# Two low parts by adding transfers, the output projection from its other half first, and another order of the second MLP chunk

## The chip, the cores and the metric

The kernel runs as one program on one core of a Trainium2 chip. Its time is the device time in microseconds (us) of one execution. Weights and activations come from device memory; layout changes of the inputs are made on the host before and are not timed. The names of the engines in the profile are PE (TensorE, matmuls), PEld (its weight loads), DVE (VectorE), ACT (ScalarE), POOL (GpSimd) and SP (SyncE, which issues most transfers).

## What is computed

A trunk of two layers over two requests, 512 and 256 tokens of 1024 features, float32. Layer 0 mixes tokens by windowed attention, layer 1 by a gated convolution of width 3; after each come an MLP with a squared ReLU (1024 to 4096 and back) and a gated embedding of the layer:

```python
for i in range(DEPTH):
    h = rms_norm(x, norm_mix[i])
    x = x + (window_attention(h, ...) if i % 2 == 0 else short_conv(h, ...))
    h = rms_norm(x, norm_mlp[i])
    x = x + jnp.square(jax.nn.relu(h @ mlp_w_up[i])) @ mlp_w_down[i]
    gate = jax.nn.sigmoid(rms_norm(x, norm_ple[i]) @ ple_w_gate[i])
    x = x + (p[i] @ ple_w_proj[i]) * gate
return rms_norm(x, final_norm)
```

The attention ends with a projection, `out @ w_o`, whose result is added to x. The change lies there, at the beginning of layer 0's MLP, and in the second chunk of both MLPs.

## The kernel before

Features lie on the 128 partitions, so x is eight blocks of 128 features by T = 768 tokens, numbered 0 to 7; H = 384 is half of the tokens. All matmuls take operands of the type float32r. To keep the accuracy, each operand is split in two: a **high part**, which is its copy in float32r, made by ACT, and a **low part**, the operand minus its high part, made by DVE. A product is then three matmuls: high by high, high by low, low by high. The groups of instructions are named by the lines that record them: L434 is the high part of a weight and L445 its low part, both 128x1024 (1024 columns hold two blocks of 512), L466 the products of seven (below), L1062 and L1166 those of the plain chunks.

**Weights.** `Weights7` holds one chunk of an up or down matrix: two raw tiles of 512 KB, which SP loads into a ring of three buffers (`fetch`, L89). In a *plain* chunk (the first two of each up matrix, `PLAIN`) the group "direct" is the first raw tile (`w11`, `w12`) and goes to the tiles `zhi` and `zlo`, of which there is one each. The group "second" is the other raw tile (`w21`, `w22`) and goes to `whi` and `wlo`, of which there are two each, shared with other weights. `high(group)` and `low(group)` make the two parts. In the other chunks a scheme of seven products in place of eight (as Strassen's) is used, which needs sums of weight blocks: `sums32` and `sums14` are two DVE additions of 128x512 each, for the groups "s32" and "s14".

**Activations.** The same scheme needs sums of x blocks m and m + 4 (`Norm7.copied`, then `Sums`: `t13` and `t42`, two DVE operations each, and `high` and `low`, twice each). `Acts` does it for the MLP's hidden blocks: `highx`, `lowx`, `t13`, `t42`, two `high`, two `low`.

**Order.** The planner of the framework orders each engine's queue by priority and an estimate of times. Inside `manual_schedule` blocks the order of ACT, PE and DVE is that of the program text. The first six blocks of the output projection (`first_head`) are left to the planner; what follows (`first_tail`, and both MLPs) is written out by hand.

**The output projection.** For block m, `output(m)` multiplies what is still missing of the heads: for m < 4 four head blocks (24 matmuls) with a weight of `w_o0`, for m >= 4 two head blocks (12 matmuls) with `w_o2` in `zhi` and `zlo`, since the rest was added during the attention (`xa`). Then `add` adds it to x, `plain_block` makes the high and low parts of x times the gain (one ACT and one DVE operation of 128x768 for m >= 4, two of 128x384 on each for m < 4), and `square` adds the block's squares to a sum. The order of the blocks is `PAIRED`: 0, 4, 1, 5, 2, 6 in `first_head` and 3, 7 in `first_tail`. After that PE computes four products `pj` for the second layer's embedding (48 matmuls), which ACT copies out.

**The first two chunks of up.** `up_first` (layer 0; layer 1 goes through the rest of `up_begun`) multiplies chunk 0 with all of x: first the half that uses "direct", then the half that uses "second". Meanwhile ACT and DVE make the reciprocal root of the mean square (`rstd_mlp`, in three steps), the sums of x blocks (`s1` to `s3`), and the parts of chunk 1 (`v`). `up_plain` does the same for chunk 1. Each result is rectified out of PSUM by DVE (`rectified`, L1021), 128x384 at a time, squared by ACT (L1024), and turned into operands by the steps of `acts_of`, which stand in the list `pend` and are taken from it by `late(n)` or in a weave. Chunk 2 is the first with seven products (`up`); its ACT copy `c` (L1225) of the first product frees PE for the third.

In `up_plain` the order of chunk 1's other work on DVE is: four steps of chunk 0's activations, then `sums32`, `sums14` and the direct split woven with the two `high` and two `low` of the activations, then the split of "s32", then the rectifications:

```python
rest, pend[:] = pend[:4], pend[4:]
weave(rest, ...)
...
sums = [] if v.plain else [v.sums32, v.sums14, lambda: v.split("direct")]
weave(norm.combine(todo.pop(0)) if todo else [], sums, pend)
...
v.split("s32")
y1, y2 = big("y1"), big("y2")
rects((0, 1), (0, 0))
squared(y1)
...
rects((1, 1), (1, 0))
```

Of the kernel before, what the change touches and what calls it, by code (L numbers as in the profile page):

```python
# [20 lines left out]
KB = D // P  # L21
# [26 lines left out]
def trunk_kernel(ctx: ExitStack, tc: tile.TileContext, a: dict, out: bass.AP):  # L48
# [38 lines left out]
    def fetch(src):  # L87
        raw = wp.tile([P, CH], F32, name="wraw", bufs=3)
        nc.sync.dma_start(raw[:, : src.shape[1]], src)  # L89
        return raw  # L90
# [80 lines left out]
    class Norm:  # L171
# [16 lines left out]
            self.square(m, xb)  # L188

        def square(self, m, xb):  # L190
            if m == 0:
                act.activation(self.acc, xb, AF.Square)
            else:
                sq = self.temp("sq")
                act.activation(sq, xb, AF.Square)
                dve.tensor_tensor(self.acc, self.acc, sq, ALU.add)
# [5 lines left out]

        aside = temp

        ready = False

        def acc_parts(self):
            ah, al = self.aside("ah", F32R), self.aside("al", F32R)
# [187 lines left out]
    class Weights7:  # L396
# [3 lines left out]
        def __init__(self, src1, src2, plain=False):  # L400
            self.plain = plain
            self.raw = [fetch(src1), fetch(src2)]
            self.w, self.parts, self.due = {}, {}, set()
            if not plain:
                self.s = [more.tile([P, CH], F32, tag=f"sum{i}", name="sum", bufs=1) for i in range(2)]
# [11 lines left out]
        def high(self, group):  # L417

            self.due.add(group)
            names = self.GROUPS[group]  # L420
            if group in ("s32", "s14"):
                src = self.s[group == "s14"][:]
            else:
                src = self.raw[group != "direct"][:, CH - 512 * len(names) :]
            n = len(names) * 512
            if group == "s32" or (self.plain and group == "direct"):
                tag = "z"
            else:
                tag = "v" if group == "w22" else None
            if tag is None:  # L430
                hi, lo = (wp.tile([P, CH], F32R, name=f"w{p}", bufs=2) for p in ("hi", "lo"))
            else:
                hi, lo = (more.tile([P, n], F32R, tag=f"{tag}{p}", name=f"{tag}{p}", bufs=1) for p in ("hi", "lo"))
            act.activation(hi[:], src, AF.Copy)  # L434
            self.parts[group] = hi, lo, src
            for i, k in enumerate(names):
                c = slice(512 * i, 512 * i + 512)
                self.w[k] = hi[:, c], lo[:, c]

        def low(self, group):  # L440
            if group not in self.due:
# [391 lines left out]
    def add(m, ps, src=None):  # L833

        src = x(m) if src is None else src
        for t, o, e in pieces(ps):
            dve.tensor_tensor(x(m)[:, o:e], src[:, o:e], t, ALU.add)
# [108 lines left out]
    def first_head(norm):  # L946


        behind, product, ws = second_inputs(xs0[24:])
        w = [weight(a["w_o0"][2], 4)] * 2  # L950
        w2 = weight(a["w_o2"], 2, tag="z")

        def output(m):
            ps = both()
            if m < KB // 2:
                group2(ps, terms_of(w[m], [p[4:] for p in aos], col=m % 2 * P))
            else:
                group2(ps, terms_of(w2, [p[6:] for p in aos], col=(m - 4) * P))
            return ps

        for i, m in enumerate(PAIRED[:6]):
            if i == 1:
                w += [weight(a["w_o0"][3], 4)] * 2
            ps = output(m)
            add(m, ps, xa[m])
            norm.block(m, x(m))
            behind(i)

        return output, product, ws

    def first_tail(norm, places, output, product, ws):

        pjs = []

        def copied(m):
            t = slot(places[m], "pjs", F32)
            for f, o, e in pieces(pjs[m]):
                act.activation(t[:, o:e], f, AF.Copy)
            nc.sync.dma_start(pj[1][KB // 2 + m], t[:])

        norm.ready = True
        c = ws[1]
        m6, m7 = PAIRED[6:]
        ps = [output(m) for m in (m6, m7)]
        pjs.extend(product(m) for m in range(KB // 2))
        add(m6, ps[0], xa[m6])
        norm.plain_block(m6, x(m6))
        norm.square(m6, x(m6))
        c.high("direct")
        add(m7, ps[1], xa[m7])  # L990
        norm.plain_block(m7, x(m7))
        c.low("direct")
        norm.square(m7, x(m7))
        copied(0)
        parts = norm.acc_parts()
        s0 = norm.copied(0, 4)
        copied(1)
        s0.t13()
        c.high("second")
        s0.high(0)  # L1000
        c.low("second")
        copied(2)
        s0.t42()
        s0.high(1)
        s1 = norm.copied(1, 5)
        copied(3)
        s0.low(0)
        s0.low(1)
        return c, up_chunk(0, 1), parts, s1

    def mlp(l, norm, nxt, w, places, early, product=None, begun=None):
# [85 lines left out]
        def up_first(ps, w, v, parts, s1):  # L1097


            nonlocal r  # L1100
            plain_block(ps[0], 0, w, range(4))
            ss = norm.sum_squares(psum, parts=parts, tag="C")
            plain_block(ps[0], 0, w, range(4, KB))
            plain_block(ps[1], 1, w)
            logs, newton, result = norm.rstd_steps(psum, ss)
            logs()
            s1.t13()
            s1.t42()
            s1.high(0)
            s1.high(1)  # L1110
            newton()
            s2 = norm.copied(2, 6)
            result()
            r = norm.r
            s1.low(0)
            s1.low(1)
            v.high("direct")
            s2.t13()
            s2.high(0)
            v.low("direct")  # L1120
            s2.t42()
            s2.high(1)
            s3 = norm.copied(3, 7)
            s2.low(0)
            s2.low(1)
            y = [big(f"y{i + 1}") for i in range(2)]
            for i in range(2):
                for o in range(2):
                    rectified(y[i], ps[i][o], H * o, H * o + H, ALU.max)
                if i == 0:  # L1130
                    s3.t13()
                    s3.high(0)
                    squared(y[0])
                    s3.t42()
                    s3.high(1)
                    v.high("second")
                    s3.low(0)
                    s3.low(1)
                    v.low("second")
            pend.extend(acts_of(0, *y, y[1]))  # L1140
            return v

        def up_plain(u, w, make, then):
# [15 lines left out]
            for n, (i, ks, sides) in enumerate(order):  # L1159
                for k in range(*ks):  # L1160
# [3 lines left out]
                    for j, (wt, part) in enumerate(((hi, 0), (hi, 1), (lo, 0))):  # L1164
                        for o in sides:
# [4 lines left out]
                                start=k == 0 and j == 0,  # L1170
                                stop=k == KB - 1 and j == 2,
                            )
                if n == 0:
                    v = make()
                    if not known and not parts:
                        parts = norm.acc_parts()
                        norm.table()
                    rest, pend[:] = pend[:4], pend[4:]
                    split2 = [lambda: v.split("second")] if v.plain else []
                    soon = v.plain and len(todo) and product  # L1180
                    weave(split2 + [lambda: v.split("direct")] if soon else [])
                    weave(rest, norm.combine(todo.pop(0)) if todo else [], [] if soon else split2)
                    if product and not known:
                        ss = norm.sum_squares(psum, parts=parts, tag="C")
                elif n == 1:
                    if not product and not known:
                        ss = norm.sum_squares(psum, parts=parts, tag="C")
                    if v.plain and not soon:
                        v.split("direct")
                    steps = [] if known else norm.rstd_steps(psum, ss)  # L1190
                    for step in steps[:1]:
                        step()
                    sums = [] if v.plain else [v.sums32, v.sums14, lambda: v.split("direct")]
                    weave(norm.combine(todo.pop(0)) if todo else [], sums, pend)
                    pend.clear()
                    for step in steps[1:]:
                        step()
                    r = norm.r
                elif n == 2:
                    if not v.plain:  # L1200
# [4 lines that stand above are left out]
                else:  # L1205
                    rects((1, 1), (1, 0))
                    pend.extend(acts_of(u, y1, y2, y2))
            return v

        def up(u, w, make, then):  # L1210
# [12 lines left out]
                late()  # L1223
            c = bank("A" if first else "C", "c")[:, :H]
            act.activation(c, a, AF.Copy)  # L1225
            late(3 if first else 1)
            w.split("w22")
            late()
            b = bank("A" if first else "B", "b")[:, :H]
# [669 lines left out]
```

## Time and profile before

| | us |
|---|---|
| median of 3 runs | 1687.13 |
| fastest and slowest of them | 1685.48, 1689.2 |
| the profiled execution, whole | 1689.38 |
| its span, first to last instruction | 1687.5 |
| output projection and `pj`, PE (layer 0) | 277 to 310.6 |
| chunk 0 of up, layer 0 | 310.8 to 328.8 |
| chunk 1 of up, layer 0 | 328.8 to 346.4 |
| chunk 2 of up, layer 0 | 346.4 to 366 |
| chunks 0, 1 of up, layer 1 | 1118.4 to 1152.5 |

How to read it: the stages are given as the times of PE's matmuls in the timeline of the profiled execution, from the span's start. A row of the timeline holds the start, the length, engine, line, operation, what is written and read, shapes and count; in brackets stand the engine's idle time before it and what ended that. A row of several instructions gives their length from the first start to the last end. The page's chain that ended last is followed back from the last instruction, at each step to what released it; its rows hold start, length, engine and tile. Matmuls overlap, so PE's idle time in the rows is somewhat less than the time lost.

### The profile page before, as it was taken

The page shows a single profiled execution, that of the slowest core. Times are in us where ns is not written, and L with a number is a line of the kernel's source. Part 1 is how long each engine was busy: PE and PEld are TensorE (multiplying, and loading weights), DVE is VectorE, ACT ScalarE, POOL GpSimd, SP SyncE. Part 2 cuts the span into 40 slices and gives each one's busy share as a digit, 9 for nine tenths or more (in the row PEclk, how much of TensorE's full clock was granted, in tenths as well). Part 3 has the DMA queues.
Part 4 walks back from the last instruction along what each step waited for, and adds up shares of the span by engine and source line. Part 5 has one row for each costly group of instructions (what it writes and reads, how often), then busy time and mean ns, then how long its engine had stood idle before and what let it go on. Part 6 is the DMA issues. An engine that isn't in the chain of part 4 may idle for free.

```text
span 1687.5 us, 24113 instructions
## 1 busy us (share of the span) xinstructions
PE 1650.1 (98%) x9410; PEld 1590.2 (94%) x9410; DVE 1415.1 (84%) x2304; ACT 903.9 (54%) x1449; POOL 18.3 (1%) x44
## 2 busy tenths in 40 slices
PE   8999999999999999999999999999999999999996
PEld 6888788989999999999999999999999999999986
DVE  6598888889999989987888877868999898998776
ACT  6377756755455455544654334545545545554544
POOL 0211000000000000000000000000000000000000
PEclk9999999999999999999999999999999999999998
DMA  8754322212221222222312222121222122122222
GB/s 261 191 153 142 95 63 82 76 63 75 66 83 64 76 71 67 74 95 72 101 60 75 76 65 77 60 74 51 75 71 80 63 76 75 63 76 88 82 75 94
DMA packets 46820, 144.60 MB, mean 86 GB/s; under 512 B 6080, under 2 KB 9152, under 8 KB 46704
## 3 DMA queue, kind: packets, MB, share of 16 engines
q1 hardware_dynamic: 45168, 139.89, 26.1%
q0 software_dynamic: 1536, 3.15, 0.8%
q8 instruction: 74, 1.21, 0.3%
q14 instruction: 42, 0.34, 0.1%
HBM read 123.10 MB, written 10.48 MB: 79 GB/s over the span
## 4 chain that ended last, share of the span: by engine, by line
PE 60%; DVE 29%; ACT 7%; issue 3%; DMA 1%; SPq 0%; DVEq 0%; ACTq 0%
PE a L466 17%; PE mm L129 9%; PE mm L138 7%; PE b L466 4%; PE gate L138 4%; PE B L466 3%; PE C L466 3%; DVE t L361 3%; DVE wlo L445 3%; DVE y L1021 3%; DVE zlo L445 2%; DVE act L394 1%; PE pt L733 1%; PE c L466 1%; ACT y L1024 1%
## 5 line engine op out<-in xcount | busy, mean ns | idle before, releaser
L434 ACT ACTIVATE whi<-sum 128x1024 fp32r<-128x1024 f32 x67 | 70.5, 1053 | 146.8 <-PE a L466 146.8
L1024 ACT ACTIVATE y<-y 128x768 f32<-128x768 f32 x64 | 53.8, 840 | 143.1 <-DVE y L1021 143.1
L466 PE MATMUL a<-xs,whi 128*128 128x384 f32 x624 | 121.9, 337 | 0.7 <-DVE low L1660 0.7
L466 PE MATMUL a<-t,zhi 128*128 128x384 f32 x536 | 109.9, 338 | 2.2 <-ACT c L1225 2.2
L466 PEld LDWEIGHTS a<-xs,whi 128*128 128x128 f32 x624 | 110.1, 188 | 1.1 <-DVE low L1660 1.1
L466 PE MATMUL a<-t,whi 128*128 128x384 f32 x536 | 108.8, 336 | 0.0
L466 PE MATMUL b<-t,zhi 128*128 128x384 f32 x536 | 108.7, 336 | 0.0
L466 PEld LDWEIGHTS a<-t,zhi 128*128 128x128 f32 x536 | 95.1, 189 | 2.7 <-ACT c L1225 2.5
L466 PE MATMUL a<-act,whi 128*128 128x384 f32 x448 | 96.6, 337 | 0.0
L445 DVE TENSOR_TENSOR wlo<-wraw,whi 128x1024 fp32r<-128x1024 f32 x72 | 87.8, 1220 | 8.7 <-ACT whi L434 8.7
L466 PEld LDWEIGHTS a<-t,whi 128*128 128x128 f32 x536 | 94.9, 188 | 0.0
L466 PEld LDWEIGHTS b<-t,zhi 128*128 128x128 f32 x536 | 94.8, 188 | 0.0
L445 DVE TENSOR_TENSOR wlo<-sum,whi 128x1024 fp32r<-128x1024 f32 x67 | 81.9, 1222 | 10.1 <-ACT whi L434 10.1
L1281 DVE TENSOR_TENSOR x<-x,a 128x384 f32<-128x384 f32 x112 | 60.8, 553 | 33.7 <-PE a L466 33.5
L434 ACT ACTIVATE zhi<-sum 128x1024 fp32r<-128x1024 f32 x67 | 71.0, 1059 | 22.8 <-DVE sum L410 22.8
L138 PE MATMUL mm<-xs_mix,whi 128*128 128x512 f32 (+1 forms) x320 | 83.1, 342 | 0.0
L445 DVE TENSOR_TENSOR zlo<-sum,zhi 128x1024 fp32r<-128x1024 f32 x67 | 81.6, 1218 | 0.0
L466 PEld LDWEIGHTS a<-act,whi 128*128 128x128 f32 x448 | 79.9, 188 | 0.0
L434 ACT ACTIVATE whi<-wraw 128x1024 fp32r<-128x1024 f32 x72 | 75.7, 1052 | 6.1 <-PE C L466 5.7
L355 ACT ACTIVATE t<-y 128x768 fp32r<-128x768 f32 x56 | 47.1, 842 | 40.3 <-DVE y L346 29.9
L466 PE MATMUL a<-xs,wlo 128*128 128x384 f32 x312 | 67.1, 336 | 0.2 <-DVE wlo L445 0.2
L466 PE MATMUL b<-t,zlo 128*128 128x384 f32 x268 | 64.1, 344 | 3.1 <-DVE zlo L445 2.0
(336 smaller groups left out, 4489.5 us busy)
## 6 DMA issues: line engine op xcount, KB each, us to landing
wraw<-in_up SPq DMA_DIRECT2D x64, 512.0 KB, 3.5
wraw<-in_down SPq DMA_DIRECT2D x64, 512.0 KB, 3.5
wraw<-in_w_in SPq DMA_DIRECT2D x24, 512.0 KB, 3.5
wraw<-in_gate SPq DMA_DIRECT2D x16, 512.0 KB, 3.5
pj<-pjs SPq DMA_DIRECT2D x16, 384.0 KB, 3.1
wraw<-in_w_q SPq DMA_DIRECT2D x8, 512.0 KB, 4.4
wraw<-in_w_out SPq DMA_DIRECT2D x8, 512.0 KB, 3.5
x_in<-in_x SPq DMA_DIRECT2D x8, 384.0 KB, 7.3
```

Of the source, the lines that this page charges most:

```text
L129: pe.matmul(t, lhsT=w, rhs=x[:, o:e], start=first and i == 0 and j == 0, stop=last and i == n - 1 and j == 2)
L138: pe.matmul(ps[:, o:e], lhsT=w, rhs=x[:, o:e], start=i == 0 and j == 0, stop=i == n - 1 and j == 2,)
L355: act.activation(t[0][:], (self.q1, self.q2)[i][:], AF.Copy)
L361: dve.tensor_tensor(lo[:], (self.q1, self.q2)[i][:], hi[:].bitcast(F32), ALU.subtract)
L394: dve.tensor_tensor(lo[:], self.q2[:], hi[:].bitcast(F32), ALU.subtract)
L434: act.activation(hi[:], src, AF.Copy)
L445: dve.tensor_tensor(lo[:], src, hi[:].bitcast(F32), ALU.subtract)
L466: pe.matmul(ps, lhsT=a, rhs=b, start=start and i == 0, stop=i == len(terms) - 1, skip_group_check=True)
L733: pe.transpose(pt[:, h * P : (h + 1) * P], lg[h // 2][:, h % 2, b * P : (b + 1) * P], ident[:],)
L1021: dve.scalar_tensor_tensor(t[:, o:e], src, 0.0, r[:, o:e], op, ALU.mult)
L1024: act.activation(t[:], t[:], AF.Square)
L1281: dve.tensor_tensor(t[:, o : o + H], t[:, o : o + H], f, op)
```

## The change

It has three parts.

1. `first_head` and `first_tail` take the blocks in the order 4, 0, 5, 1, 6, 2, then 7, 3, where it was 0, 4, 1, 5, 2, 6, then 3, 7. The first block's squares start the sum, whichever block it is (`begun`).
2. A new function, `added(group)`, makes the two parts of a weight without DVE: ACT makes the high part, ACT writes the negated high part into the low tile, and POOL issues a transfer that reads the raw weight from device memory once more (512 KB) and adds it to the low tile. It takes the place of `high` and `low` for "second" of chunk 0 in `first_tail` (now ahead of the last block's parts; before among the first sums of x) and for "second" of chunk 1 in `up_first` (now right behind the reciprocal root; before at the end, between the rectifications).
3. In `up_plain`, chunk 1 of both layers has its own order: `sums32` ahead of the hidden blocks' parts, the direct split and the split of "s32" between their steps, the first rectifications ahead of the last `high`, `sums14` behind them, and the last two `low` steps handed on to chunk 2, which takes them by `late(5)` in place of `late(3)`.

```diff
 def square(self, m, xb):
-    if m == 0:
+    if not self.begun:
+        self.begun = True
         act.activation(self.acc, xb, AF.Square)
...
 class Weights7:
         self.raw = [fetch(src1), fetch(src2)]
+        self.src = src1, src2
...
+    def added(self, group):
+        self.high(group)
+        self.due.remove(group)
+        hi, lo, _ = self.parts[group]
+        act.activation(lo[:], hi[:].bitcast(F32), AF.Copy, scale=-1.0)
+        nc.gpsimd.dma_start(lo[:], self.src[group == "second"], accum_op=ALU.add)
...
 # first_head
-for i, m in enumerate(PAIRED[:6]):
+order = [m ^ KB // 2 for m in PAIRED]
+for i, m in enumerate(order[:6]):
...
 # first_tail
-m6, m7 = PAIRED[6:]
+m6, m7 = KB - 1, KB // 2 - 1
...
 c.high("direct")
 add(m7, ps[1], xa[m7])
+c.added("second")
 norm.plain_block(m7, x(m7))
 c.low("direct")
...
 s0.t13()
-c.high("second")
 s0.high(0)
-c.low("second")
 copied(2)
...
 # up_first
 result()
 r = norm.r
+v.added("second")
 s1.low(0)
 s1.low(1)
 v.high("direct")
...
 s3.high(1)
-v.high("second")
 s3.low(0)
 s3.low(1)
-v.low("second")
...
 # up_plain, after the matmuls of each quarter n of the chunk
-if n == 0:
+if begun and n == 0:
+    v = make()
+elif begun and n == 1:
+    steps, pend[:] = pend[:], []
+    steps[0]()
+    v.sums32()
+    steps[1]()
+    steps[2]()
+    v.split("direct")
+    steps[3]()
+    steps[4]()
+    v.split("s32")
+    y1, y2 = big("y1"), big("y2")
+    rects((0, 1), (0, 0))
+    steps[5]()
+    v.sums14()
+    squared(y1)
+elif begun and n == 2:
+    rects((1, 1))
+elif begun:
+    rects((1, 0))
+    pend.extend(steps[6:] + acts_of(u, y1, y2, y2))
+elif n == 0:
...
 # up, chunk 2 is "first"
-late(3 if first else 1)
+late(5 if first else 1)
```

## What is forecast

> **What bounds the kernel now.** I read the page first, then the waits of PE between 270 and 380 us, the timeline there, the granted clock by windows, and the chain that ended last in that stretch. Of the page three lines matter.
>
> ```profile
> span 1687.5 us, 24113 instructions
> PE 1650.1 (98%) x9410; PEld 1590.2 (94%) x9410; DVE 1415.1 (84%) x2304; ACT 903.9 (54%) x1449; POOL 18.3 (1%) x44
> ...
> PE 60%; DVE 29%; ACT 7%; issue 3%; DMA 1%; SPq 0%; DVEq 0%; ACTq 0%
> ```
>
> TensorE sets the time nearly everywhere, so this change, which leaves every matmul in place, can win only where TensorE waits. All the places that it touches lie in the first layer's head and in the second chunk of each MLP. PE's own waits there (engine, line, what it waited for: us in total, times, longest):
>
> ```profile
> PE a L466 <- ACT c L1225: 2.2, 1, 2.2
> PE mm L129 <- ACT whi L83: 1.1, 1, 1.1
> PE p L1166 <- DVE wlo L445: 0.6, 1, 0.6
> PE b L466 <- DVE zlo L445: 0.5, 1, 0.5
> PE ss L235 <- ACT pjs L978: 0.3, 1, 0.3
> PE a L466 <- DVE wlo L445: 0.2, 1, 0.2
> ```
>
> That is 4.9 us, but it is not the whole loss. The second layer runs the same matmuls through the same two plain chunks and half of the third, and shows what they take unhindered. The timeline has both:
>
> ```profile
> 310.79 0.34 PE L1062 MATMUL p<-xs,zhi 128*128 128x384 f32 x1
> 354.20 2.30 PE L466 MATMUL a<-t,zhi 128*128 128x384 f32 x8 [2.16 <-ACT c L1225]
> 360.03 1.56 PE L466 MATMUL a<-t,whi 128*128 128x384 f32 x8
> 1118.38 0.34 PE L1062 MATMUL p<-xs,zhi 128*128 128x384 f32 x1
> 1156.66 1.55 PE L466 MATMUL a<-t,zhi 128*128 128x384 f32 x8
> 1160.84 1.56 PE L466 MATMUL a<-t,whi 128*128 128x384 f32 x8
> ```
>
> From the first up matmul to the fifth product of the third chunk, 244 matmuls: layer 0 takes 360.03 - 310.79 = 49.24 us, layer 1 1160.84 - 1118.38 = 42.46 us. So layer 0 loses **6.78 us**. Of that, 5.83 - 4.18 = 1.65 us lie behind the longest gap, where the 24 matmuls from 354.20 on run slowly. The windows say why (busy time and count of PE, PEld, DVE, ACT, POOL, then granted clock, DMA share, GB/s):
>
> ```profile
> 352.00:354.20 2.20, 0.04 (x1) 0.00 (x1) 1.27 (x3) 2.20 (x4) 0.00 (x0) 1.00 0.00 0
> 354.20:358.50 4.30, 4.30 (x16) 4.30 (x17) 3.77 (x6) 3.43 (x7) 0.00 (x0) 0.60 0.02 4
> 1152.40:1160.80 8.40, 8.40 (x50) 8.40 (x49) 6.27 (x11) 6.29 (x10) 0.00 (x0) 1.00 0.01 1
> ```
>
> After the 2.16 us gap the granted clock is 0.60 for 4.3 us; layer 1, without a gap, stays at 1.00. I count the slow stretch as part of the gap's price. The Trainium skill (TensorE: Matmul & The Clock Gate, Part 1: The HAM clock gate) says that the array falls to half rate after about 3.4 us of idleness; this trace differs, with 2.16 us of idle ahead of the drop.
>
> Who makes PE late is told by the chain that ended last. From 300 us to the gap it holds no matmul, only VectorE, ScalarE and the steps between them:
>
> ```profile
> 305.08 0.94 DVE x L837 x2
> 306.04 0.95 ACT xs L309
> ...
> 310.07 0.84 ACT ah L83
> ...
> 313.32 0.95 ACT whi L434
> ...
> 314.30 1.23 DVE wlo L445
> ...
> 337.05 1.22 DVE wlo L445
> 338.27 0.94 DVE y L1021 x2
> ...
> 348.06 1.82 DVE t L361 x2
> ...
> 353.68 0.48 ACT c L1225
> ```
>
> Both removed subtractions (314.30 and 337.05) stand on it, and so do the two low parts of the activations (348.06) that the new order moves.
>
> **The change part by part.** I followed the two engines' queues by hand, each instruction starting when its engine and its inputs are free, with the spacings of the rows (the x2 rows give 0.91 for a 128x768, 0.47 for a 128x384; single rows 1.2 and 0.95 for a 128x1024 on DVE and ACT).
>
> *Order of the output projection.* The matmuls are the same. The last block becomes 3 (24 matmuls) in place of 7 (12 matmuls), so DVE has about 4.2 us between the last two blocks instead of 2.1 us and is done with block 7 when block 3 comes out, at the time when block 7 came out before. Its addition starts at 303.3 instead of 305.0. At the start, PE waits until 277.15 (first row below); the profile names ACT's `whi`, which isn't an operand of the first output. The other event there is DVE's last reading of the attention's PSUM:
>
> ```profile
> 277.15 0.65 PEld L129 LDWEIGHTS mm<-aos,whi 128*128 128x128 f32 x4 [1.22 <-ACT whi L83]
> 276.61 0.42 DVE L767 TENSOR_TENSOR xa<-xa,mm 128x256 f32<-128x256 f32 x1
> 323.66 0.96 DVE L267 SCALAR_TENSOR_TENSOR rstd_mlp<-v,y 128x768 f32<-128x768 f32 x1
> 340.53 0.56 DVE L391 TENSOR_TENSOR act<-y,act 128x384 fp32r<-128x384 f32 x1 [1.32 <-ACT act L381]
> 345.72 0.68 DVE L414 TENSOR_TENSOR sum<-wraw 128x512 f32<-128x512 f32 x1
> 350.93 1.94 DVE L1021 SCALAR_TENSOR_TENSOR y<-p,rstd_mlp 128x384 f32<-128x384 f32 x4
> ```
>
> That reading ends at 277.03, 0.12 us before PE goes on, and a new pool in the same banks has to wait for it whichever block is first. So this wait's end is worth 0 to 1.05 us; I take 0, the row nearest to it being the PSUM reading, and keep 1.05 as a rival.
>
> *First low part by transfer.* DVE loses one 1.2 us subtraction. ACT gets one more 128x1024 copy (0.95), and both copies now stand ahead of block 3's high parts. They wait for block 3's matmuls (the buffer), so they run from 303.1 to 305.1 while DVE adds block 3; the high parts behind them start at 305.1, against 306.04 for block 7 before. From there ACT's 0.95 and DVE's 1.2 at 313.32 and 314.30 are gone from the chain: the squares' high part comes at 308.9 (310.07 before), the reciprocal root at 320.9 (323.66 before), **2.8 us** earlier (1.2 + 0.95 + 1.2, less 0.6 because the sum of squares, PE's four matmuls before it, comes no earlier).
>
> *Second low part by transfer.* ACT's two copies now stand behind the root, ahead of the direct high part, at 322.9 to 324.9, and give 0.95 of that back: the direct low part gains 1.4. Then ACT's copy and DVE's 1.2 us at 337.05 are gone, and the second pair of rectifications starts at 335.4 instead of 338.27, again **2.8 us**.
>
> *Second chunks' order.* The two half sums (s32) go into DVE's wait of 1.32 us for ACT. The two low parts (1.82) and the other two half sums (two of 0.6 to 0.7) go behind the first rectification. So that comes at 343.7, against 350.93: 2.8 + 1.3 + 1.8 + 1.2 = 7.1 us earlier. The square and ACT's split of s14 follow by 347, and the copy `c` waits for PE alone. PE, which at 42.46/244 = 0.174 us a matmul reaches the third chunk at 310.79 + 196 x 0.174 = 345.0, finds each operand ready up to the fifth product: all 6.78 us are gone there, the slow clock with them.
>
> What is late next: the two deferred low parts must be paid in the third chunk, 1.8 us, and DVE has no idle time there. The next place at which PE needs DVE is the second product of the first down step:
>
> ```profile
> 369.22 0.62 PE L466 MATMUL b<-t,zlo 128*128 128x384 f32 x2
> 1170.30 0.62 PE L466 MATMUL b<-t,zlo 128*128 128x384 f32 x2 [0.19 <-DVE zlo L445]
> 1156.43 0.56 DVE L391 TENSOR_TENSOR act<-y,act 128x384 fp32r<-128x384 f32 x1 [0.96 <-ACT act L381]
> ```
>
> By my chain this `zlo` is done at 363.5, about 1.1 us after PE wants it (100 matmuls behind 345.0), and of that 0.15 us are lost on the `wlo` before. PE goes on at 363.55 instead of 369.22, 5.7 us earlier. The same chain over the old order gives 368.75 for that 369.22, so the difference of the two chains is 5.2 us. I take **5.3 us**.
>
> In layer 1 PE has no wait in these chunks to lose. DVE is earlier there too, but its last rectification has to wait for PE's matmuls, so it gains no lead; the split of s14 moves ahead of them by half a us, the deferred low parts fill what is left of the idle 0.96 us ahead of 1156.43 (last row), and the `zlo` at 1170.30 comes out within 0.1 us of before. I cost layer 1 at 0; without that cover it would be the 1.8 us of the two low parts.
>
> *The transfers themselves.* No row shows an adding transfer. The nearest are these (size, median us from issue to landing):
>
> ```profile
> wraw<-in_up SPq DMA_DIRECT2D x64, 512.0 KB, 3.5
> bias<-skew POOLq DMA_DIRECT2D x32, 96.0 KB, 5.3
> ```
>
> POOL has no other work here; nothing is queued behind the wait for ACT's negated copy but the second transfer. Landing lies between 3.5 us, as SP's load of this size, and 5.3 x 512/96 = 28 us, if POOL's 96 KB scale with size. I take 7 us: POOL's issue costs 5.3 - 3.5 = 1.8 more than SP's, and reading the old contents about half of 3.5 more. The users are these:
>
> ```profile
> 320.48 0.33 PE L1062 MATMUL p<-xs,whi 128*128 128x384 f32 x1
> 337.18 0.52 PE L1166 MATMUL p<-x,whi 128*128 128x384 f32 x2
> ```
>
> The low part comes two matmuls after each. By my chain the first transfer can start at 305.2 and is needed at 320.2, 15 us; the second starts at 325.0 and is needed at 337.0, 12 us. At 7 us both are free. If the second takes longer than 12 us, PE waits for it directly. The raw tiles come free earlier, so SP's next loads go out earlier; DMA's share there is low and I count nothing.
>
> **The rivals.**
> - *The transfer is late.* It speaks for it that an adding transfer is unmeasured and the 28 us bound is above both covers. Against it: POOL is idle and the transfer has 12 us, more than three plain loads. It decides from 12 us on; each us more costs one. The gain is used up at about 17 us, and at 28 us the kernel is slower by 11 us: about 1698 us. Chance 0.05.
> - *The head's chain gets little shorter.* ACT gains two 0.95 us copies at places where DVE waits for ACT, and the first six blocks' order on DVE and ACT isn't written out, so the planner may place them otherwise. Then only the second chunks' order counts: the gap at 354.20 shrinks without the head's 2.8 us, and DVE's debt at the down step stays. That leaves 2 to 4 us, 1684.1 us. Chance 0.21.
> - *The slow clock stays.* If the clock of 0.60 is not the gap's doing, the slow 4.3 us remain somewhere in this stretch when the gap is gone: 5.3 - 1.65 = 3.65, 1683.5 us. That it stands right behind the only gap of this length, and nowhere in layer 1's windows, speaks against it. Chance 0.05. (The rule of the Trainium skill named above would have it so, the gap being shorter than its 3.4 us.)
> - *The start's wait goes too*, if PE did wait for ACT's `whi` at 277.1: 1.05 us more, 1680.8 us. Chance 0.07.
>
> **How the numbers follow.** The profiled execution took 1689.38 us, 1.9 around its span, and lies 2.25 us above the median, at the upper edge of the runs (1685.48 to 1689.2); 5.3 us are the same from either. From the median 1687.13 the forecast is **1681.8 us**, chance 0.62, with its own range of 1680 to 1683.5. The range to 8 in 10 takes in the start's wait and a run's scatter below, and most of the second rival above: 1679.5 to 1686. Some 0.2% (3.4 us) is what a measurement of this kernel can tell from no change. Faster by more than that: the forecast nearly whole (0.59), the start's wait (0.07), a quarter of the second rival and half of the third (0.08), 0.74. Within: 0.21. Slower: 0.05.
>
> **What would show it.** Right: no wait of PE on ACT `c` near 352 us, granted clock 1.00 there; 244 matmuls from the first up product in 42.5 to 43 us; a wait of about 1 us on DVE `zlo` in the first down step, where layer 0 now has none; the rstd_mlp row near 321; layer 1's `zlo` wait unchanged at 0.2; adding transfers landing in 4 to 12 us. Wrong: PE waiting on a DMA at the second half of either plain chunk; DVE still behind at its first rectification of the second chunk; a gap with a slow clock left in the third; a changed wait near 277.

## The result and the profile after

The changed kernel takes **1681.78 us** (median of 8 runs, 1681.13 to 1684.55), the kernel before in the same comparison 1686.68 us (8 runs, 1685.48 to 1689.2). The ratio is 0.9975 with a 95% interval of 0.9966 to 0.9984, a gain of 2.7 to 5.7 us. The forecast was 1681.8 us, so the total came out as forecast. The steps did not all do so, and two errors met.

The page of the changed kernel, its span, its busy line and the shares of its chain:

```profile
span 1682.2 us, 24112 instructions
PE 1645.5 (98%) x9410; PEld 1586.8 (94%) x9410; DVE 1411.9 (84%) x2302; ACT 905.8 (54%) x1451; POOL 20.3 (1%) x46
...
PE 58%; DVE 30%; ACT 7%; issue 3%; DMA 1%; SPq 0%; DVEq 0%; ACTq 0%
```

Two DVE instructions have gone, two on ACT and two POOL transfers have come. The waits of PE between 270 and 380 us:

```profile
PE a L476 <- DVE y L1279: 1.7, 1, 1.7
PE mm L129 <- ACT whi L83: 1.0, 1, 1.0
PE b L476 <- DVE zlo L455: 0.4, 1, 0.4
PE p L1175 <- DVE zlo L455: 0.3, 1, 0.3
```

The 2.2 us wait on ACT `c` is gone and so are most of the small ones; a new one of 1.7 us on DVE has come, which the prediction does not have. The windows at the place of the old gap and of the slow clock:

```profile
352.00:354.20 2.20, 2.20 (x15) 2.20 (x14) 2.17 (x4) 0.38 (x1) 0.00 (x0) 1.00 0.00 0
354.20:358.50 4.30, 3.50 (x20) 3.17 (x19) 4.23 (x8) 3.01 (x4) 0.00 (x0) 1.00 0.39 122
```

PE works through the first and the clock is 1.00 in both. In its place DVE has hardly any idle time left. The timeline gives the order in which things happen now, in both layers:

```profile
276.85 0.94 PE L129 MATMUL mm<-aos,zhi 128*128 128x384 f32 x4 [1.00 <-ACT whi L83]
...
302.95 1.05 ACT L436 ACTIVATE zhi<-wraw 128x1024 fp32r<-128x1024 f32 x1
303.90 1.04 ACT L436 ACTIVATE whi<-wraw 128x1024 fp32r<-128x1024 f32 x1
304.98 1.06 ACT L447 ACTIVATE wlo<-whi 128x1024 fp32r<-128x1024 f32 x1
305.94 0.60 ACT L305 ACTIVATE xs<-x,vec 128x384 fp32r<-128x384 f32 x1
...
309.76 0.85 ACT L83 ACTIVATE ah<-acc_mlp 128x768 fp32r<-128x768 f32 x1 [1.08 <-DVE acc_mlp L197]
310.21 0.34 PE L1072 MATMUL p<-xs,zhi 128*128 128x384 f32 x1
...
321.37 0.96 DVE L268 SCALAR_TENSOR_TENSOR rstd_mlp<-v,y 128x768 f32<-128x768 f32 x1
...
323.23 0.94 ACT L327 ACTIVATE q<-x,vec 128x768 f32<-128x768 f32 x1 [0.60 <-DVE t L362]
324.08 1.04 ACT L436 ACTIVATE whi<-wraw 128x1024 fp32r<-128x1024 f32 x1
325.15 1.06 ACT L447 ACTIVATE wlo<-whi 128x1024 fp32r<-128x1024 f32 x1
326.12 1.04 ACT L436 ACTIVATE zhi<-wraw 128x1024 fp32r<-128x1024 f32 x1
327.19 1.23 DVE L455 TENSOR_TENSOR zlo<-wraw,zhi 128x1024 fp32r<-128x1024 f32 x1 [1.99 <-ACT zhi L436]
...
336.67 1.02 DVE L1031 SCALAR_TENSOR_TENSOR y<-p,rstd_mlp 128x384 f32<-128x384 f32 x2
...
345.02 1.02 DVE L1031 SCALAR_TENSOR_TENSOR y<-p,rstd_mlp 128x384 f32<-128x384 f32 x2
...
353.33 1.55 PE L476 MATMUL a<-t,whi 128*128 128x384 f32 x8
...
358.77 0.55 DVE L1279 TENSOR_TENSOR y<-a,p 128x384 f32<-128x384 f32 x1
359.37 1.66 PE L476 MATMUL a<-xs,whi 128*128 128x384 f32 x8 [1.68 <-DVE y L1279]
...
364.90 0.61 PE L476 MATMUL b<-t,zlo 128*128 128x384 f32 x2 [0.38 <-DVE zlo L455]
...
1113.74 0.34 PE L1072 MATMUL p<-xs,zhi 128*128 128x384 f32 x1
1156.31 1.56 PE L476 MATMUL a<-t,whi 128*128 128x384 f32 x8
1165.77 0.62 PE L476 MATMUL b<-t,zlo 128*128 128x384 f32 x2 [0.20 <-DVE zlo L455]
```

The reader is to see three things. ACT makes three copies of a weight tile in a row, from 302.95 and from 324.08 on. The first time block 3's high parts stand behind all three; the second time the last of the three, `zhi`, is itself what DVE waits for: at 327.19 DVE has idled 1.99 us for it. The new wait at 359.37 is the chunk's seventh product, which goes into PSUM bank `a` again once DVE has read it. And the 244 matmuls from the first up product to the fifth product of the third chunk take 353.33 - 310.21 = 43.12 us (49.24 before); layer 1's take 1156.31 - 1113.74 = 42.57 (42.46 before).

**A measure for small differences.** Executions of one kernel differ by 2 to 3 us, mostly ahead of the projection. The stretch itself repeats far better, so I count from the projection's first matmul to the second product of the first down step (`b<-t,zlo` in the timeline): 369.22 - 277.18 = 92.04 us before, 364.90 - 276.85 = 88.05 after. The change takes **4.0 us** out of the stretch that it touches; a second execution of each, below, gives 92.04 and 88.20, so 3.8 us. The stretch resolves some 0.2 us where the total resolves 1 to 2. Most of the 0.15 us between the changed kernel's two executions arises in the projection: from its first matmul to the first up product PE takes 33.36 us in one (310.21 - 276.85) and 33.61 in the other, without a wait, and the times behind it are 0.15 us later. It takes 33.61 in both executions of the kernel before, and below in the rows "chunks' order alone", "changed, old chunks' order" and "first transfer only" and in the last variant of all; in the others it takes 33.35. What causes it stays open. Differences of 0.2 us between rows of the two kinds tell nothing.

### The profile page after: what moved, and what is told of

The parts are those of the page before. It is cut to its first block, busy times and chain, and to the rows that moved or that the text cites. A ratio compares the mean times of both kernels' runs of the same rounds, so it can differ in the third digit from the quotient of the medians.

```text
span 1682.2 us, 24112 instructions
## 1 busy us (share of the span) xinstructions
PE 1645.5 (98%) x9410; PEld 1586.8 (94%) x9410; DVE 1411.9 (84%) x2302; ACT 905.8 (54%) x1451; POOL 20.3 (1%) x46
## 4 chain that ended last, share of the span: by engine, by line
PE 58%; DVE 30%; ACT 7%; issue 3%; DMA 1%; SPq 0%; DVEq 0%; ACTq 0%
PE a L476 17%; PE mm L129 9%; PE mm L138 8%; PE b L476 4%; PE B L476 4%; PE C L476 3%; DVE t L362 3%; DVE wlo L455 3%; DVE y L1031 3%; PE gate L138 3%; DVE zlo L455 2%; DVE act L395 1%; PE pt L743 1%; DVE sum L412 1%; ACT y L1034 1%
## 5 line engine op out<-in xcount | busy, mean ns | idle before, releaser
L455 DVE TENSOR_TENSOR vlo<-wraw,vhi 128x512 fp32r<-128x512 f32 x67 | 46.1, 689 | 24.8 <-ACT vhi L436 24.8
```

What stands on the lines that cost most here:

```text
L455: dve.tensor_tensor(lo[:], src, hi[:].bitcast(F32), ALU.subtract)
```

## The experiments

Each kernel ran beside the kernel before, whose median was 1686.68 us beside the changed kernel, 1686.09 beside the first three runs below and "direct high part first", 1685.84 beside "first transfer only", "first copies behind" and the first two runs of the down steps, and 1685.47 beside the rest; the ratios are to it. "Stretch" is the time just defined, from that kernel's profile; the other columns are times after the projection's first matmul, from the same timelines (start of the squares' high part `ah`, of the reciprocal root, of the first chunk's direct `zlo`, of the second pair of rectifications).

| kernel | median us | ratio to before, 95% | `ah` | root | `zlo` | rect. | stretch |
|---|---|---|---|---|---|---|---|
| before | 1686.68 | | 32.89 | 46.48 | 50.26 | 61.01 | 92.04 |
| changed | 1681.78 | 0.9966 to 0.9984 | 32.92 | 44.52 | 50.35 | 59.82 | 88.05 |
| chunks' order alone | 1683.17 | 0.9977 to 0.9995 | 32.89 | 46.49 | 50.27 | 61.03 | 89.26 |
| changed, old chunks' order | 1684.44 | 0.9979 to 0.9996 | 33.06 | 44.67 | 50.49 | 59.96 | 91.01 |
| changed, no transfers | 1681.10 | 0.9962 to 0.9983 | 31.73 | 45.32 | 49.10 | 59.85 | 88.07 |
| changed, first transfer only | 1681.02 | 0.9965 to 0.9986 | 33.06 | 44.68 | 48.46 | 59.22 | 87.45 |
| changed, direct high part first | 1681.06 | 0.9956 to 0.9981 | 32.92 | 44.53 | 48.32 | 58.24 | 86.48 |
| ... and first copies behind | 1680.64 | 0.9957 to 0.9980 | 32.57 | 44.19 | 47.98 | 57.90 | 86.13 |

### Which part carries the gain

*The chunks' order alone*, in the kernel before:

```diff
+if begun and n == 0:
+    v = make()
+elif begun and n == 1:
...
-late(3 if first else 1)
+late(5 if first else 1)
```

> The kernel before with the second chunks' new order alone; both second-group low parts are again DVE subtractions and the projection keeps its old order. Theory A (the whole chain of DVE and ACT from the projection's last block to the first down step sets the time, and each part counts by what it takes off that chain): the first rectification of the second chunk comes 1.3 + 1.8 + 1.2 = 4.3 us earlier than before (350.9 to about 346.6), PE's 2.16 us gap at ACT c goes, the waits near 315 and 338 us stay, and the zlo of the first down step comes 1.5 to 2.5 us earlier, as only DVE's idle time there is saved. Time 1.5 to 2.5 us below before. Theory B (the second chunks' order alone carries the gain, the two transfers and the projection's order bring nothing): as the changed kernel, 4.4 to 5.4 us below before.

Measured: 1683.17 us; the stretch is 92.04 - 89.26 = 2.8 us shorter, and up to the second rectifications every time is that of before to 0.02 us. The gap at `c` is gone; PE waits 1.7 us at the seventh product instead. A little above theory A's 1.5 to 2.5, and far from B's 4.4 to 5.4: the order is the largest part, but not the whole.

*The changed kernel without the chunks' order* (its lines taken back):

> The changed kernel with the second chunks' old order (projection's order and both adding transfers stay). Theory A: the first rectification of the second chunk comes about 1.3 to 1.6 us earlier than before, so the gap of 2.16 us at ACT c shrinks to between 0.5 and 1.2 us, and the granted clock behind it stays above 0.60; the zlo of the first down step comes earlier by the two subtractions taken off DVE, less what DVE idles. Time 1.5 to 3 us below before. Theory B: within 0.7 us of before.

Measured: 1684.44 us, 1.65 below before; the stretch is 1.0 us shorter. The median lies in theory A's 1.5 to 3 us, but the stretch doesn't, and A's mechanism, a gap that shrinks, misses; B's 0.7 us is missed too. The projection and the transfers make the second rectifications 1.05 us earlier, and PE, with two small waits fewer, comes to the third chunk as much earlier. So the gap does not shrink (its row, then the window behind it):

```profile
350.28 0.96 PE L476 MATMUL a<-t,zhi 128*128 128x384 f32 x4 [2.17 <-ACT c L1234]
```

```profile
350.20:354.50 4.30, 4.22 (x24) 4.22 (x25) 3.76 (x6) 3.48 (x8) 0.00 (x0) 1.00 0.02 4
```

The same gap, and the clock behind it is 1.00. The two results give the chunks' order 2.8 us alone and 91.01 - 88.20 = 2.8 us on top of the rest (88.20 is the changed kernel's execution with the same 33.61 us of projection). So 2.8 and 1.0 add up to the change's 3.8.

*The changed kernel without the transfers*, both low parts subtracted on DVE again where they stood:

```diff
-c.added("second")
...
+c.high("second")
 s0.high(0)
+c.low("second")
...
-v.added("second")
...
+v.high("second")
 s3.low(0)
 s3.low(1)
+v.low("second")
```

> The changed kernel with both second-group low parts made by DVE's subtraction again, where they stood (projection's order and second chunks' order stay). Theory A: DVE pays 1.2 us twice ahead of the first down step, so PE's waits on DVE at the third chunk's seventh product and at zlo are together about 2 us longer than in the changed kernel: 2.5 to 3.5 us below before. Theory B: the transfers bring nothing, 4.4 to 5.4 us below before.

Measured: 1681.10 us, stretch 88.07 against the changed kernel's 88.05. Theory A falls as far as the transfers go: **together they bring nothing**. They are not late, and they do take DVE's subtractions away. The table's rows show where the gain goes. Without them `ah` comes 1.2 us earlier than with them (31.73 against 32.92), because ACT's copies no longer stand ahead of block 3's high parts. The saved subtraction and copy then make the root 0.8 us earlier with them (44.52 against 45.32). At `zlo` they are 1.25 us behind again (50.35 against 49.10), since the second tile's copies stand ahead of `zhi`, and the second saved subtraction makes the rectifications level (59.82 and 59.85). Against the kernel with the chunks' order alone, this run gives the projection's order 89.26 - 88.07 = 1.2 us, nearer 1.0 as the first of the two has the longer 33.61 us of projection. So theory B's time came, but not all that it says: this order does bring something.

### Is it the place of ACT's copies?

From here the theory was that each transfer takes work off DVE, but that its copies stand in the wrong place of ACT's queue. *Only the first transfer*, the second tile as before:

```diff
-v.added("second")
...
+v.high("second")
 s3.low(0)
 s3.low(1)
+v.low("second")
```

> The changed kernel with only the first adding transfer; the first chunk's second low part is a DVE subtraction again, where it stood. Theory F (formed from the last runs: each transfer takes a 1.22 us subtraction and a 0.95 us copy off the chain, but its two ACT copies stand ahead of a high part on which DVE waits; the first comes out 0.8 us to the good at the reciprocal root, the second 0.8 us to the bad at the second rectifications): zlo of the first chunk comes near 48.3 us after the projection's first matmul (50.35 in the changed kernel, 49.10 without transfers), the second rectifications near 59.0 (59.82, 59.85), PE's wait on DVE at the third chunk's seventh product is 0.8 us shorter than the 1.7 us: 0.8 us below the changed kernel. Rival G (the transfers bring nothing because DVE's lag is made up later whatever is taken off): within 0.2 us of the changed kernel in the stretch.

Measured: the stretch is 87.45, 0.6 us below the changed kernel, and `zlo` and the rectifications are 1.9 and 0.6 us earlier. (This run has the longer 33.61 us of projection; against 88.20, the changed kernel's execution that has it too, the effect is 0.75.) PE's wait at the seventh product is 1.38 us, only 0.3 shorter and not the expected 0.8, as PE also comes to it 0.3 us earlier. The stretch fits theory F and not G: leaving out the second transfer is better than having it where it stands.

*The direct high part first:*

```diff
-v.added("second")
 s1.low(0)
 s1.low(1)
 v.high("direct")
+v.added("second")
```

> The changed kernel with one thing moved: in the first chunk of the first layer the high part of the direct group goes on ACT ahead of the second group's high part, negated copy and adding transfer, no longer behind them. Theory A: in the changed kernel DVE idles 1.99 us at 325.2 for that high part, which two ACT copies hold up; with it first, zlo there is done about 2 us earlier, PE's wait of 0.3 us on it goes, the second rectifications come near 335 instead of 336.7, and PE's wait on DVE at the third chunk's seventh product (1.7 us) falls below 0.5 us: 1.5 to 2.2 us below the changed kernel. The transfer starts about 1 us later, near 327.7, and lands near 335 where PE needs it at 336.9. Rival D (DVE's lag comes from elsewhere, what it gains there it idles later): less than 0.5 us from the changed kernel. Rival E (the transfer becomes late): PE waits on a DMA near 337 us.

Measured: 1681.06 us. The stretch is 86.48, 1.6 us below the changed kernel; the median, over 5 runs, does not show it. ACT and DVE at the place:

```profile
323.51 1.04 ACT L436 ACTIVATE zhi<-wraw 128x1024 fp32r<-128x1024 f32 x1
324.46 1.04 ACT L436 ACTIVATE whi<-wraw 128x1024 fp32r<-128x1024 f32 x1
325.53 1.06 ACT L447 ACTIVATE wlo<-whi 128x1024 fp32r<-128x1024 f32 x1
```

```profile
324.59 1.23 DVE L455 TENSOR_TENSOR zlo<-wraw,zhi 128x1024 fp32r<-128x1024 f32 x1
```

DVE's idle 1.99 us is gone; `zlo` comes 2.0 us earlier (48.32), the rectifications 1.6. The rest of PE's wait at the seventh product is 0.65 us, a little over what was expected. Theory A's mechanism holds here, rival D falls, and there is no wait on a DMA (E).

*And the first tile's copies behind the last block's square:*

```diff
-c.added("second")
 norm.plain_block(m7, x(m7))
 c.low("direct")
 norm.square(m7, x(m7))
+c.added("second")
```

> As the run with the direct high part first, and the first transfer's high part and copy moved too, behind the last block's square. Theory F: the squares' high part comes 1.2 us earlier (31.7 us after the projection's first matmul instead of 32.9), the reciprocal root near 43.3, zlo of the first chunk near 47.1, the second rectifications near 57.1, and PE's wait on DVE at the third chunk's seventh product (0.7 us there) goes; what is left in the stretch is the wait on zlo in the first down step, 0.4 us or less: 0.7 to 1.2 us below that run, 2.2 to 2.8 below the changed kernel. Rival G: no change against that run. The first transfer starts near 309 and lands near 316, needed at 320.

Measured: 1680.64 us, stretch 86.13. Only 0.35 us of the 0.7 to 1.2 came. The block's part was right, DVE's first `zlo` is 1.2 us earlier, but the two copies now stand ahead of `ah` itself, which comes at 32.57 and not 31.7: I had moved them past one thing that is waited for and in front of the next.

### The wait that is left in every down step

Each of the 14 down steps behind an up chunk has a wait of PE on `zlo`: the rows show 0.38 us of idle time in the first (at 364.90) and at most 0.21 in the others, each costing PE 0.3 to 0.55 us from start to start. *`zlo` ahead of the chunk's last two rectifications:*

```diff
 dve.tensor_tensor(y2[:, :H], d, p, ALU.add)
+if seven:
+    v.low("s32")
 rectified(y2, y2[:], 0, T, ALU.min)
```

> The changed kernel with the low part of s32 (zlo) of each down step that follows an up chunk issued on DVE ahead of the chunk's last two rectifications, 1.5 us earlier. If PE's 0.38 to 0.48 us at zlo in each of these steps (seven in each layer) is DVE's order alone, all of them go: 0.65 + 6 x 0.40 + 7 x 0.47 = 6.3 us below the changed kernel. If the rectifications, 1.2 us later, hold up the next copies on ACT and so PE, they come back as another wait: within 2 us of the changed kernel.

Measured: **1709.14 us**, ratio to before 1.0138 (1.0123 to 1.0152): 23 us slower than before, and outside both expectations. The waits on `zlo` went, but each step gained larger ones. ACT and PE in the first step:

```profile
363.88 0.85 ACT L1034 ACTIVATE y<-y 128x768 f32<-128x768 f32 x1 [5.47 <-DVE y L1031]
364.63 1.04 ACT L436 ACTIVATE whi<-sum 128x1024 fp32r<-128x1024 f32 x1
365.57 0.83 ACT L1034 ACTIVATE y<-y 128x768 f32<-128x768 f32 x1
366.31 0.84 ACT L1309 ACTIVATE C<-a 128x384 f32<-128x384 f32 x2
```

```profile
PE a L476 <- ACT C L1309: 17.6, 14, 1.3
PE a L476 <- ACT c L1256: 7.2, 12, 0.6
```

The copy `C`, for which PE waits, stands on ACT behind a square that needs the rectification. *With all three moves together:*

> Both ACT moves and the early zlo together. If they add: 2.2 to 2.8 and 5 to 6 us, so 7 to 9 us below the changed kernel, 12 to 14 us below before, with no wait of PE over 0.3 us left between 300 us and the end of the first down step. If PE then meets another wait of DVE in the third chunk: 5 to 7 us below the changed kernel.

Measured: 1705.63 us, ratio 1.0119 (1.0105 to 1.0134). Neither expectation holds; it is the same loss, 3.5 us smaller. *`zlo` between the two rectifications*, so that the square keeps its place (`v.low("s32")` behind `squared(y2)`):

> The changed kernel with the low part of s32 (zlo) in each down step that follows an up chunk issued between the chunk's last two rectifications: it is 0.47 us earlier, the first of the two (whose square stands ahead on ACT) keeps its place and only the last one, 0.55 us long, comes 1.2 us later. If that last rectification has room (its square starts near 365.0 in the first such step, after ACT's copy of s14, and the rectification would end at 364.9): PE's waits of 0.38 to 0.48 us at zlo go nearly whole, 4 to 6 us below the changed kernel. If it hasn't: the copies C come later, PE waits for them as in the run with zlo ahead of both, and the time is level with the changed kernel or above it.

Measured: 1680.93 us, ratio 0.9972 (0.9962 to 0.9983), level with the changed kernel. The stretch is 0.5 us shorter (361.48 - 273.91 = 87.57). In the next down step PE and ACT show why no more came:

```profile
421.16 0.83 ACT L1034 ACTIVATE y<-y 128x768 f32<-128x768 f32 x1
...
421.89 0.85 ACT L1309 ACTIVATE C<-a 128x384 f32<-128x384 f32 x2
422.41 0.65 PEld L476 LDWEIGHTS a<-t,zhi 128*128 128x128 f32 x4 [0.40 <-ACT C L1309]
422.41 0.97 PE L476 MATMUL a<-t,zhi 128*128 128x384 f32 x4
```

PE comes to that product with no wait for `zlo`, about 0.25 us before the copy `C` lets it write (its last two matmuls begin at 421.82, so at the usual 0.17 us for each this one would start at 422.17, not at 422.41), and gives most of the gain back there. Two chains, DVE to `zlo` and ACT to `C`, end within 0.3 us of each other. *With both ACT moves as well:*

> The same in the kernel with both ACT moves. If the two add: 1.9 us from the stretch of the first layer's head and 4 to 6 us from the down steps, 6 to 8 us below the changed kernel; otherwise as the run without the ACT moves.

Measured: 1679.90 us (5 runs), ratio 0.9965 (0.9952 to 0.9977), stretch 360.45 - 274.65 = 85.80, 2.25 us below the changed kernel (2.4 below its execution with the same projection). It is the best by the stretch of all that gain in the total too; its median is 5.6 us below that of the kernel before beside it, where the changed kernel's is 4.9 below, and the intervals overlap. The 4 to 6 us expected of the down steps did not come.

### The clock, and how well the stretch repeats

> The kernel before once more, for its clock: if the gap of 2.16 us ahead of the third chunk's third product sets off the slow clock, the granted clock is about 0.60 again in the 4.3 us behind it; the run with the second chunks' old order had the same gap at 1.00, so I expect either. If the slow clock is hidden by DVE's lag, the first down step's wait on zlo ends at 92.0 us after the projection's first matmul with it or without it.

The rows of the gap and of the seventh product, and the window behind the gap, in this second execution of the kernel before:

```profile
351.54 0.79 PE L466 MATMUL a<-t,zhi 128*128 128x384 f32 x3 [2.17 <-ACT c L1225]
361.04 1.67 PE L466 MATMUL a<-xs,whi 128*128 128x384 f32 x8 [0.83 <-DVE y L1248]
```

```profile
351.50:355.80 4.30, 4.26 (x24) 4.26 (x25) 3.76 (x6) 3.48 (x7) 0.00 (x0) 1.00 0.02 4
```

The gap is the same and the clock is 1.00. And yet the stretch is 366.56 - 274.52 = 92.04 us, that of the execution with the slow clock: here PE reaches the chunk's seventh product earlier and waits 0.8 us for DVE, which it did not before. The slow clock cost the stretch nothing.

> The changed kernel once more: the seventh product of the third chunk at 82.5 and the second product of the first down step at 88.05 us after the projection's first matmul, within 0.2 us, whatever the rest of the execution does.

Measured: 88.20 for the second product, the same to 0.15 us, though this execution took 1681.58 us and the one above 1684.2. That 2.6 us lies outside the stretch.

## Why the prediction was right, and where its steps were not

*The total.* Forecast 5.3 us from 1687.13; the stretch gives 4.0. The base was 0.45 us high (1686.68 over 8 runs), and the medians' difference of 4.9 us stands 0.9 above the stretch's 4.0, within its interval. So the exact hit at 1681.8 is in part luck: by the stretch the sum of the steps is 1.3 us too large.

*The order of the projection.* Forecast: `ah` 1.2 us earlier, with the first transfer in place. In fact `ah` did not move (32.89 and 32.92). The order alone, without transfers, does give 1.2 us at `ah` and at the root, and 1.2 us of the stretch (some 1.0 each without the 0.15 us of the two kinds of execution). The failed step is "they run from 303.1 to 305.1 while DVE adds block 3; the high parts behind them start at 305.1": there are three copies, `zhi` at 302.95 ahead of the two, and the high part starts at 305.94. The end of PE's wait near 277 stayed as forecast, at 0 gain: the first output now reads `zhi`, and PE still goes on at 276.85, 0.11 us after DVE's last reading of the attention's PSUM:

```profile
276.33 0.41 DVE L777 TENSOR_TENSOR xa<-xa,mm 128x256 f32<-128x256 f32 x1
```

*First low part by transfer.* Forecast 2.8 us at the root, measured 1.96 (46.48 to 44.52). The saved subtraction and copy are real: from `ah` to the root it is 11.6 us now and 13.6 before, 2.0 shorter where the forecast had 1.6. But the 1.2 us that it counted on at `ah` are lost to the copies.

*Second low part by transfer.* The step that failed most is "the direct low part gains 1.4". (Its own terms, 2.8 less 0.95, would give 1.85; the rest is not named.) It lost 0.1 (50.26 to 50.35). The copies were to start at 322.9, right behind the root, and to give back 0.95. ACT could take them only at 324.08, behind a `q` that waits for DVE (row at 323.23), and both of them, 2.04 us, stood ahead of `zhi`. The second rectifications came 1.2 us earlier, not 2.8. Moving two lines brought 1.6 of that back.

*Second chunks' order.* Forecast 1.3 + 1.8 + 1.2 = 4.3 us at the first rectification: in the run with this part alone it came at 346.43 - 277.05 = 69.38, against 350.93 - 277.18 = 73.75 before, 4.4 us. Right. All parts together bring it to 345.02 - 276.85 = 68.17, 5.6 us earlier where 7.1 were forecast, and the missing 1.5 us are those of the two low parts above.

*What is late next.* Of the 6.78 us up to the fifth product 6.1 went (49.24 to 43.12; 42.5 to 43 was named as the sign), nearly all, as forecast. Behind it the place was wrong: PE needs DVE not first at the down step's second product but at the chunk's seventh, for the PSUM bank that DVE's `y` has to read (1.68 us at 359.37). Which of the two PE meets first changes little, as DVE works through 19.45 of the 20 us from 345 to 365 and sets both:

```profile
345.00:365.00 20.00, 17.94 (x102) 17.30 (x100) 19.45 (x30) 10.89 (x16) 0.00 (x0) 1.00 0.24 79
```

The rule that DVE's `zlo`, not the gap, sets the gain was right: `zlo` starts at 363.63 - 276.85 = 86.78 against 367.95 - 277.18 = 90.77, and PE's second product moved by the same 4.0.

*The 6.78 us and the slow clock.* "I count the slow stretch as part of the gap's price" was wrong: with the same gap and no slow clock the kernel before takes the same 92.04 us. DVE's lag hid it. The rule of the Trainium skill that the prediction cited (TensorE: Matmul & The Clock Gate, Part 1: The HAM clock gate) has a half that I left out: the window over which activity is judged runs freely, so the point at which the clock changes differs between executions (the Trainium skill says it of the warm-up). This fits one execution of three with this gap; the 2.16 us against its 3.4 us stay unexplained here.

*Layer 1* was costed at 0: its run from the first up product to the first down step's second takes 1165.77 - 1113.74 = 52.03 us, 1170.30 - 1118.38 = 51.92 before.

*The transfers' time.* Estimated 7 us; measured (tile, queue, count, size, median from issue to landing):

```profile
wlo<-in_up POOLq DMA_DIRECT2D x2, 512.0 KB, 6.6
```

The two were issued at 306.5 and 326.7, and PE read the tiles from 320.0 and 336.9 on: covers of 13.5 and 10.2 us, where 15 and 12 were forecast. So they are hidden, as forecast; in no run did PE wait on one.

*The rivals.* The second, that the head's chain gets little shorter because of ACT's copies, named the right mechanism: of 2.8 us forecast at the rectifications 1.2 came. It let only the second chunks' order count and so priced the gain at 2 to 4 us; that order gives 2.8, and the projection's order brings 1.0 to 1.2 more without the transfers. The stretch's 4.0 stands at the upper end of this rival, and the total's interval of 2.7 to 5.7 us does not separate it from the forecast: the number alone does not show that the working was right.

## What to carry to other kernels

Work taken off one engine and given to another is paid at the place where the new instruction stands in the other's queue: two ACT copies of 1 us, with ten us to spare for their transfer, cost all that the transfer saved by standing one step too early. Follow the engine that works without a pause, and ask for each of its results which engine meets it first; a gap of PE is worth only what that engine gains, and the slow clock behind it was worth nothing here, as that engine's lag filled the time. Where effects are below 0.2%, measure between two marked instructions of the trace: the stretch told 0.5 us apart, where the medians did not tell 1.6.

## What was not expected of the hardware

An adding transfer of 512 KB landed in 5.4 to 7.7 us over the runs, not far above POOL's 96 KB (5.3 in the kernel before) and about twice SP's plain load of the same size (3.5), and POOL was held 0.9 us by each issue. The granted clock behind one and the same gap of 2.16 us was 0.60 in one execution and 1.00 in two others.
